# The last FFN's sums of h^T taken by token tiles ahead of its norm, and the context's turn set between the last channel products

## The chip, the core and the metric

The kernel runs on one core of a Trainium2 chip. Its time is the device time of one launch in microseconds (us). The engines are named as in the profile: PE is TensorE (PEld its weight loads), DVE VectorE, ACT ScalarE, POOL GpSimd, and SP the queue from which all transfers are issued, in a fixed order.

## The reference, cut to what matters

One layer of a diffusion backbone on 1024 latent tokens and 256 context tokens, with 1024 channels: a SwiGLU FFN, a token mixer (Fourier heads beside a two-way state-space scan, started from states that the context gives), and a second FFN. Each sublayer has a norm before and after.

```
def macaron_ffn(x, mod3, norm_pre, norm_post, w_gate, w_up, w_down):
    h = modulate(rms_norm(x, norm_pre), mod3[:, 0], mod3[:, 1])
    y = (silu(h @ w_gate) * (h @ w_up)) @ w_down
    return x + 0.5 * mod3[:, 2] * rms_norm(y, norm_post)

x, ctx = macaron_ffn(x, ...ffn1), macaron_ffn(ctx, ...ffn1)
h_f, h_b = context_states(ctx, ...)          # final scan states of the context
x = mix_sublayer(x, h_f, h_b, ...)           # input projection, conv, scan, output projection
return macaron_ffn(x, ...ffn2)
```

## The kernel before

Every fp32 operand is split into a high and a low fp32r part (ACT casts the high part, L198; DVE or POOL subtracts it for the low part, L199), and a product is three matmuls, high by high, high by low, low by high (`mm3`, L461). Tokens are worked in 8 tiles of 128. Before each large product the normed tokens are scaled, turned by PE transposes (`pre_turn`: L813, then L818 on ACT and L820 on DVE, L825 and L826 for the parts) and kept as h^T.

The order of instructions on each engine is fixed when the program is built, by a scheduler that works from its own estimate of durations; an instruction then waits only for semaphores. SP issues transfers in its own order too: a transfer that waits holds up all that stand behind it.

Two places matter here. First, `project` ends with ten channel products (`pch`, 96 matmuls of 512 columns, with convolutions L946 to L949, and for six of them transposes `pxt`, copied at L1065). After the last, `ssd_and_ctx` turns the two context tiles `cx` and starts the context's first FFN (`gu`, 256 columns), into whose steps the scan's chunks (`pcb`, `pD`, `pbt`) are mixed.

Second, `mix_out` runs over the 8 token tiles: scan, output projection (`pwo`), `post` (norm, residual, x2 written to DRAM), `pre` (norm and turn into h3, also written to DRAM as `h3_d`, L823). The last FFN's gate and up products use a seven-product scheme in place of eight for all but the first two column blocks: it needs the plain h^T blocks and four sums T1 to T4 of them. The first two blocks (weights `wfirst`) are plain products, 192 matmuls `gu`, and so can run while the sums are made. For this `ffn2` reads h3 back from DRAM (L1653 and the next line) in four chunks i through two buffers `hb`, sums (`h_sums`, L396 to L399), casts (L416) and subtracts (L422). Then `uload` (L527) brings the first weights of the scheme into a ring in the bank F0, `usums` (L534 to L537) and `usplit` prepare them, and the products `pa` to `pd` start. In the trace, F is the bank F0, h_d is h3_d, x_d is x1_d or x2_d.

Of the kernel before, what the change touches and what calls it, by code (L numbers as in the profile page):

```python
# [7 lines left out]
F32 = mybir.dt.float32  # L8
FR = mybir.dt.float32r
# [118 lines left out]
class Kernel:  # L128
# [263 lines left out]
    def h_sums(self, hb):  # L392

        m, V = self.m, self.nc.vector
        b = [m.f(hb, 512 * q, 512 * q + 512) for q in range(7)]
        V.tensor_tensor(out=b[4], in0=b[2], in1=b[3], op=ALU.add)  # L396
        V.tensor_tensor(out=b[3], in0=b[3], in1=b[0], op=ALU.subtract)
        V.scalar_tensor_tensor(out=b[5], in0=b[2], scalar=-1.0, in1=b[3], op0=ALU.mult, op1=ALU.subtract)
        V.tensor_tensor(out=b[6], in0=b[1], in1=b[5], op=ALU.add)  # L399

    def h_split(self, i, hb, highs, lows, first):

# [548 lines left out]
    def project(self):  # L951
# [90 lines left out]
        self.xs = m.alloc(8 * 768, F32, self.X)  # L1042
        acc = Ring(m, 1024, 2)
        xc = Ring(m, 1024, 2)
        cts = list(range(10, 14)) + list(range(4, 10))
        for ct in cts:
            w = self.weights(a["w_ch"][2 + ct], 1024)
            P = self.psum("pch")

            for cs in (((0, 1),) if ct != cts[-1] else ((0,), (1,))):  # L1050
                self.chan_proj(P, w, hT, cs)
            ac = m.f(acc.next())
            if ct >= 10:
                T, g = self.BT, ct - 10
                dst = m.f(T).rearrange("p (c g l) -> p c g l", g=4, l=128)[:, :, g, :]
                self.conv(P, 1024, ct, ac, dst, ac.rearrange("p (c l) -> p c l", l=128))
            else:
                x_ = m.f(xc.next())
                self.conv(P, 1024, ct, ac, x_)
                for h in range(2):  # L1060
                    P = self.psum("pxt", "D")
                    for c in range(4):
                        nc.tensor.transpose(out=P[:, 128 * c : 128 * c + 128], in_=x_[:, 512 * h + 128 * c : 512 * h + 128 * c + 128], identity=self.ident())
                    dst = m.f(self.xs).rearrange("p (c j) -> p c j", j=768)[:, 4 * h : 4 * h + 4, (ct - 4) * 128 : (ct - 4) * 128 + 128]
                    V.tensor_copy(out=dst, in_=P.rearrange("p (c j) -> p c j", j=128))  # L1065
            if ct == 10:

                self.cx, junk = [m.alloc(1024) for _ in range(2)], m.alloc(1024)
                for t in range(2):
                    self.load(self.cx[t], a["ctx"][t * 128 : t * 128 + 128, :])  # L1070
                    self.pre_scale(m.f(self.cx[t]), self.cx[t], junk)
                m.free(junk)
        acc.release()
        xc.release()
        self.whi, self.wlo = whi, wlo
        m.free(*self.hh, *self.hl)
        self.wrelease()

    def softplus(self, x, n):
# [262 lines left out]
    def ssd_and_ctx(self):  # L1342
        m, nc, a = self.m, self.nc, self.a
        V, S = nc.vector, nc.scalar
        self.rs = nc.vector
        self.y_d = self.dram([8, 128, 768], "y_d")
        self.s_d = self.dram([2, 8, 128, 768], "s_d")
        hh, hl = m.alloc(2048, FR), m.alloc(2048, FR)
        self.wrings(3, 3)
        for r in (self.whi, self.wlo):  # L1350
            r.areas = r.areas[1:] + r.areas[:1]
        full = Ring(m, 512, 2)
        for t in range(2):
            self.pre_turn(1, m.r(hh), m.r(hl), 256, t * 128, self.cx[t], full, "main")
        full.release()
        m.free(*self.cx)
# [24 lines left out]

        for j in range(NG):
            more = j < NG - 1
            self.g1_one(wa, hT, g[0], 0)
            if more:
                wa = self.weights(w1[2 * j + 2])
            slot()
            self.g1_one(wb, hT, g[1], 0)
            if more:
                wb = self.weights(w1[2 * j + 3])  # L1390
            slot()
            for t in range(2):
# [105 lines left out]
    def mix_out(self):  # L1498
# [12 lines left out]
        wo = self.wo  # L1511
        m.free(m.sub(self.ct, 0, 512))
        F0, Q = self.F0, self.Q
        yr, zr, hr = Ring(m, 768, 1, F32, F0), Ring(m, 768, 2, F32, Q), Ring(m, 768, 3, F32, Q)
        xb, x1 = Ring(m, 1024, 1, F32, F0), Ring(m, 1024, 2, F32, F0)
        Gm = self.gload(2)
        full = Ring(m, 512, 1, F32, F0)
        tr, ft = Ring(m, 384, 3, F32, F0), Ring(m, 256, 1, F32, Q)
# [69 lines left out]
        full.areas.append(m.alloc(512, F32, F0))  # L1588
        P = xx = None
        for c in range(8):  # L1590
            fo, f0 = fr.next(), ft.next()
# [21 lines left out]

        (X1, X2) = self.cut("x", (12288, FR), (1536, F32))
        self.X1, self.X2 = X1, X2
        self.whi, self.wlo = Pairs(), Pairs()
        for b in (R0, X1):
            for r in (self.whi, self.wlo):
                r.areas.append(m.alloc(2048, FR, b))
        self.raw = Ring(m, 1024, 3, F32, Q)  # L1620
        w1 = a["ffn2_w1"]
        self.wfirst = [self.weights(w1[0]), self.weights(w1[1])]
        (h0, l0), (h1, l1) = h3
        gu = self.psum("gu")
        for half in range(2):
            for k in range(8):
                self.g_half_k(gu, self.wfirst[0], ((h0, h1), (l0, l1), 512), 0, k, (half,))
        self.gfirst = gu
        pre(7, post(7, P))
        for r in (xb, x1, full, self.raw):  # L1630
            r.release()
        m.free(Gm)
        (self.Q,) = self.cut("q", (Q_WORDS, FR))


    def ffn2(self):
# [20 lines left out]

        s0 = m.alloc(1024, F32, F0)
        self.banks(main=4)
        hT = ((h0, h1), (l0, l1), 512)  # L1660
        for c in range(2):
            for q in range(2):
                P = self.gfirst if (c, q) == (0, 0) else self.psum("gu")
                if (c, q) != (0, 0):
# [7 lines left out]
        m.free(s0, *hb)  # L1672
# [15 lines left out]
        def tail():  # L1688
# [6 lines left out]
            self.gring.areas = [tuple(m.sub(x, o, 384) for x in T[0]) for o in (0, 384)]  # L1695
# [4 lines left out]
        self.ffn_up(False, tail)  # L1700
        for r in (self.ut, self.sg):
            r.release()
        m.free(self.cc, wb, lb, h0, l0, h1, l1, *(x for q in T[1:] for x in q), *(m.sub(x, 768, 1280) for x in T[0]))
# [131 lines left out]
```

## Time and profile before

| | us |
|---|---|
| median of 3 runs | 2336.15 (2334.01 to 2337.88) |
| the profiled execution, its own time | 2346.82 |
| its span in the trace | 2344.8 |
| PE busy | 2168.8, 92% of the span |
| DVE / ACT / POOL busy | 1505.1 / 924.3 / 422.6 |

The span is read from the first instruction to the last; 2.0 us of the execution lie around it. PE's idle time is 176 us, and the mean granted clock is 0.966.

### The profile page before, as it was taken

The page shows a single profiled execution, that of the slowest core. Times are in us where ns is not written, and L with a number is a line of the kernel's source. Part 1 is how long each engine was busy: PE and PEld are TensorE (multiplying, and loading weights), DVE is VectorE, ACT ScalarE, POOL GpSimd, SP SyncE. Part 2 cuts the span into 40 slices and gives each one's busy share as a digit, 9 for nine tenths or more (in the row PEclk, how much of TensorE's full clock was granted, in tenths as well). Part 3 has the DMA queues.
Part 4 walks back from the last instruction along what each step waited for, and adds up shares of the span by engine and source line. Part 5 has one row for each costly group of instructions (what it writes and reads, how often), then busy time and mean ns, then how long its engine had stood idle before and what let it go on. Part 6 is the DMA issues. An engine that isn't in the chain of part 4 may idle for free. (4 is left out here: it accounts for less than half of the span.)

```text
span 2344.8 us, 28370 instructions
## 1 busy us (share of the span) xinstructions
PE 2168.8 (92%) x10532; PEld 1805.8 (77%) x10532; DVE 1505.1 (64%) x2226; ACT 924.3 (39%) x1403; POOL 422.6 (18%) x444
## 2 busy tenths in 40 slices
PE   5799999999999899998899987888799999999998
PEld 3577778887778799887888877666688888878886
DVE  6999886656645513348887866787556565656453
ACT  4322223234535433326556545356222222245341
POOL 1100000000212000007776631673000000001010
PEclk9799999999999999999999989999899999999999
DMA  6344553228755501312455445453412222258572
GB/s 259 112 136 153 169 175 99 96 84 276 251 181 192 174 28 47 105 46 90 139 165 178 145 135 166 136 182 122 153 57 85 77 87 75 88 185 275 180 228 88
DMA packets 124827, 329.39 MB, mean 140 GB/s; under 512 B 12928, under 2 KB 43776, under 8 KB 123664
## 3 DMA queue, kind: packets, MB, share of 16 engines
q1 hardware_dynamic: 124688, 327.57, 42.8%
q8 instruction: 83, 1.36, 0.2%
q14 instruction: 56, 0.46, 0.1%
HBM read 273.77 MB, written 53.76 MB: 140 GB/s over the span
## 5 line engine op out<-in xcount | busy, mean ns | idle before, releaser
L198 ACT CAST R<-F 128x1024 fp32r<-128x1024 f32 (+1 forms) x172 | 164.3, 961 | 242.5 <-PE pd L461 75.1
L199 DVE TENSOR_TENSOR R<-F,R 128x1024 fp32r<-128x1024 f32 (+1 forms) x155 | 196.3, 1271 | 79.4 <-ACT R L198 72.7
L207 POOL TENSOR_SCALAR F<-F 128x1 f32<-128x1 f32 x18 | 4.2, 235 | 1279.7 <-ACT F L228 1279.7
L198 ACT CAST Q1a<-F 128x1024 fp32r<-128x1024 f32 (+1 forms) x115 | 129.3, 1130 | 225.8 <-PE pd L461 102.7
L461 PE MATMUL pch<-R 128*128 128x512 f32 (+1 forms) x912 | 172.2, 349 | 13.8 <-DVE X3b L790 4.7
L461 PEld LDWEIGHTS pch<-R 128*128 128x128 f32 x912 | 148.1, 198 | 33.9 <-issue 10.3
L461 PE MATMUL gu<-R 128*128 128x256 f32 (+1 forms) x1152 | 162.2, 299 | 2.7 <-ACT R L198 1.2
L461 PEld LDWEIGHTS gu<-R 128*128 128x128 f32 x1152 | 149.8, 194 | 11.2 <-ACT R L198 1.6
L199 DVE TENSOR_TENSOR Q1a<-F,Q1a 128x1024 fp32r<-128x1024 f32 x93 | 113.5, 1220 | 39.0 <-ACT Q1a L198 38.8
L1253 POOL TENSOR_TENSOR R<-F 128x384 fp32r<-128x384 f32 x128 | 128.6, 1033 | 24.2 <-PE pD L1287 17.5
L461 PE MATMUL y<-Q1a 128*128 128x512 f32 x438 | 107.7, 395 | 0.0
L461 PE MATMUL pa<-R,Q1a 128*128 128x512 f32 x330 | 95.6, 401 | 10.9 <-ACT Q1a L198 9.6
L461 PE MATMUL pa<-R 128*128 128x512 f32 x306 | 87.5, 403 | 14.1 <-ACT R L198 13.3
L461 PE MATMUL y<-Q1a,X3a 128*128 128x512 f32 x360 | 93.2, 404 | 5.5 <-DVE X3b L790 2.6
L768 DVE SCALAR_TENSOR_TENSOR X3b<-X3b,F 128x512 f32<-128x512 f32 x126 | 95.1, 770 | 4.2 <-DMA X3b<-adaR 3.9
L461 PEld LDWEIGHTS y<-Q1a 128*128 128x128 f32 x438 | 83.3, 191 | 18.2
L198 ACT CAST X7a<-F 128x1024 fp32r<-128x1024 f32 (+1 forms) x47 | 57.8, 1231 | 90.9 <-PE pd L461 78.5
L461 PE MATMUL pc<-R,Q1a 128*128 128x512 f32 x286 | 87.6, 401 | 0.7 <-DVE F L604 0.7
L461 PEld LDWEIGHTS y<-Q1a,X3a 128*128 128x128 f32 x360 | 68.9, 193 | 22.9 <-issue 3.0
L461 PE MATMUL pd<-R,Q1a 128*128 128x512 f32 x286 | 84.9, 393 | 0.0
L461 PEld LDWEIGHTS pa<-R,Q1a 128*128 128x128 f32 x330 | 62.1, 191 | 29.1 <-ACT Q1a L198 12.1
L199 DVE TENSOR_TENSOR X7a<-F,X7a 128x1024 fp32r<-128x1024 f32 (+1 forms) x47 | 68.1, 1451 | 24.7 <-ACT X7a L198 24.6
(424 smaller groups left out, 4911.1 us busy)
## 6 DMA issues: line engine op xcount, KB each, us to landing
F<-ffn_wd SPq DMA_DIRECT2D x154, 512.0 KB, 4.3
F<-ffn_w SPq DMA_DIRECT2D x42, 1024.0 KB, 5.4
X3b<-adaR SPq DMA_DIRECT2D x112, 256.0 KB, 2.9
F<-ffn_w SPq DMA_DIRECT2D x44, 512.0 KB, 4.4
F<-w_ch SPq DMA_DIRECT2D x26, 512.0 KB, 4.1
g_d<-X3b SPq DMA_DIRECT2D x22, 512.0 KB, 2.7
g_d<-F SPq DMA_DIRECT2D x20, 512.0 KB
X3b<-g_d SPq DMA_DIRECT2D x44, 192.0 KB, 5.8
```

Of the source, the lines that this page charges most:

```text
L198: nc.scalar.copy(out=m.r(hi, off, off + n), in_=m.f(src, soff, soff + n))
L199: (E or nc.vector).tensor_tensor(out=m.r(lo, off, off + n), in0=m.f(src, soff, soff + n), in1=m.f(hi, off, off + n), op=ALU.subtract)
L207: V.tensor_scalar(out=mv, in0=ss, scalar1=scale * RSQ_M, scalar2=EPS * RSQ_M, op0=ALU.mult, op1=ALU.add)
L461: self.nc.tensor.matmul(out=outs[c], lhsT=l, rhs=r[c], start=first and ps == 0, stop=last and ps == 2, skip_group_check=again)
L768: V.scalar_tensor_tensor(out=ac, in0=m.f(x), scalar=s, in1=ac, op0=ALU.mult, op1=ALU.add)
L1253: G.tensor_tensor(out=m.r(R, 384 * i, 384 * i + 384).rearrange("p (h l) -> p h l", h=3), in0=self.cst(tri).unsqueeze(1).broadcast_to([128, ...
```

## The change

The context tiles are loaded and scaled before the channel products. The last two channel products are done for the first 512 tokens, then the first half of h^T is freed, the turned context takes its room, and the second 512 tokens follow; the turn stands between them.

In `mix_out`, the sums T1 to T4 are formed there, for the first three token tiles of each half (384 columns) through one buffer of five areas, and for the last pair (tiles 3 and 7) straight from the turn's buffers. The raw weights of the first two blocks come through one area in the bank X2 (X7b) and one in F0, since Q holds the sums. The second block's first product is done here too. The diff, cut to its core:

```diff
+    def t_sums(self, b):
+        V = self.nc.vector
+        V.tensor_tensor(out=b[4], in0=b[2], in1=b[3], op=ALU.add)
+        V.tensor_tensor(out=b[3], in0=b[3], in1=b[0], op=ALU.subtract)
+        V.scalar_tensor_tensor(out=b[2], in0=b[2], scalar=-1.0, in1=b[3], op0=ALU.mult, op1=ALU.subtract)
+        V.tensor_tensor(out=b[1], in0=b[1], in1=b[2], op=ALU.add)
+    def t_split(self, T, src, q, c, n):
...
+        nc.scalar.copy(out=hi, in_=src)
+        nc.vector.tensor_tensor(out=lo, in0=src, in1=hi.bitcast(F32), op=ALU.subtract)
     def project(self):
...
+        self.cx, junk = [m.alloc(1024) for _ in range(2)], m.alloc(1024)
+        for t in range(2):
+            self.load(self.cx[t], a["ctx"][t * 128 : t * 128 + 128, :])
+            self.pre_scale(m.f(self.cx[t]), self.cx[t], junk)
...
+        last = [(ct, self.weights(a["w_ch"][2 + ct], 1024), self.psum("pch")) for ct in cts[-2:]]
+        for ct, w, P in last:
+            self.chan_proj(P, w, hT, (0,))
+        m.free(self.hh[0], self.hl[0])
+        self.chh, self.chl = m.alloc(2048, FR), m.alloc(2048, FR)
+        self.cw = m.alloc(2048, FR), m.alloc(2048, FR)
+        full = Ring(m, 512, 2)
+        for t in range(2):
+            self.pre_turn(1, m.r(self.chh), m.r(self.chl), 256, t * 128, self.cx[t], full, "CB")
...
+        for ct, w, P in last:
+            self.chan_proj(P, w, hT, (1,))
+            conv(ct, P)
     def ssd_and_ctx(self):
...
-        for t in range(2):
-            self.pre_turn(1, m.r(hh), m.r(hl), 256, t * 128, self.cx[t], full, "main")
     def mix_out(self):
...
+        self.T = [(m.alloc(2048, FR, b), m.alloc(2048, FR, b)) for b in (self.Q, self.Q, X1, X1)]
-        self.raw = Ring(m, 1024, 3, F32, Q)
+        self.raw = Ring(m, 1024, 1, F32, X2)
+        self.raw.areas.append(m.alloc(1024, F32, F0))
         w1 = a["ffn2_w1"]
         self.wfirst = [self.weights(w1[0]), self.weights(w1[1])]
...
+        self.gfirst = [self.psum("gu")]
+        first(0, 0)
+        first(0, 1)
+        hb = m.alloc(5 * 384, F32, F0)
+        for i in range(4):
+            v = m.f(hb).rearrange("p (q c) -> p q c", c=384)
+            nc.sync.dma_start(out=v[:, 0:4:3], in_=self.h3_d[4 + i].rearrange("p (s c) -> p s c", s=2)[:, :, 0:384])
+            nc.sync.dma_start(out=v[:, 1:3], in_=self.h3_d[i].rearrange("p (s c) -> p s c", s=2)[:, :, 0:384])
+            self.t_sums([v[:, q] for q in range(5)])
+            self.t_split(self.T[i], v[:, 1:5], 0, 0, 384)
+        m.free(hb)
+        hb = m.alloc(3 * 512, F32, X2)
+        for q, k in ((0, 4), (1, 0)):
+            nc.sync.dma_start(out=m.f(hb, 512 * q, 512 * q + 512).rearrange("p (k c) -> p k c", k=4),
+                              in_=self.h3_d[k : k + 4, :, 384:512].rearrange("k p c -> p k c"))
+        xx = post(7, P)
+        self.gfirst.append(self.psum("gu"))
+        first(1, 0)
+        f = [full.areas[(full.i + q) % 2] for q in range(2)]
+        pre(7, xx)
+        b = [m.f(hb, 0, 512), m.f(hb, 512, 1024), m.f(f[0]), m.f(f[1]), m.f(hb, 1024, 1536)]
+        self.t_sums(b)
+        for i in range(4):
+            for q in range(4):
+                self.t_split(self.T[i], b[1 + q][:, 128 * i : 128 * i + 128].rearrange("p (q c) -> p q c", q=1), q, 384, 128)
+        first(1, 1)
     def ffn2(self):
...
-        T = [(m.alloc(2048, FR, b), m.alloc(2048, FR, b)) for b in (Q, Q, X1, X1)]
-        hb = [m.alloc(3584, F32, F0) for _ in range(2)]
         for i in range(4):
-            b = hb[i % 2]
-            nc.sync.dma_start(out=m.f(b, 0, 2048).rearrange("p (s c) -> p s c", s=4)[:, 0:4:3, :], in_=self.h3_d[4 + i].rearrange("p (s c) -> p s c", s=2))
-            self.load(b, self.h3_d[i], 512, 1536)
-            self.h_sums(b)
-            self.h_split(i, b, [(3, 7, T[i][0])], [(3, 7, T[i][1])], 3)
+            for q, op in enumerate(("T4", "T2", "T1", "T3")):
+                self.hop[op][i] = at(T[i][0], q), at(T[i][1], q)
```

The order in which instructions stand, before and in the change (built, not run). PE, end of the channel products and start of the context's FFN, before:

```order
L461 MATMUL pch<-R_60 128x512 x45
L1063 MATMUL pxt<-F_61 128x128 x8
L461 MATMUL pch<-R_60 128x512 x5
L813 MATMUL ptr<-F_61,X5a 128x128 x4
L1267 MATMUL pcb<-Q4a,X5a 128x128 x4
L813 MATMUL ptr<-F_61,X5a 128x128 x8
L1063 MATMUL pxt<-F_61,X5a 128x128 x8
L813 MATMUL ptr<-F_61,X5a 128x128 x4
L1287 MATMUL pD<-R_60 128x384 x4
L461 MATMUL gu<-R_60 128x256
L1287 MATMUL pD<-R_60 128x384 x5
L461 MATMUL gu<-R_60 128x256 x11
```

The same place in the change:

```order
L477 MATMUL pch<-R_60 128x512 x17
L829 MATMUL ptr<-F_61,X5a 128x128 x4
L477 MATMUL pch<-R_60 128x512 x28
L829 MATMUL ptr<-F_61,X5a 128x128 x4
L477 MATMUL pch<-R_60 128x512 x7
L477 MATMUL gu<-R_60 128x256 x12
L1080 MATMUL pxt<-F_61 128x128 x8
L1300 MATMUL pcb<-Q4a,X5a 128x128 x4
L477 MATMUL gu<-R_60 128x256 x40
L1080 MATMUL pxt<-F_61,X5a 128x128 x8
L477 MATMUL gu<-R_60 128x256 x23
```

The four groups of transposes `ptr` stood behind the last `pch`; the last two of them now stand within the last products (the other two stand earlier), and `gu` follows the last `pch` at once.

SP, from the last writes of h3 to the first weights of the scheme (L527), before:

```order
L823 DMA h_d<-F_61 128x4x128 x3
L1653 DMA F_61<-h_d 128x2x512 x2
L1671 DMA g_d<-F_61 128x512
L184 DMA F_61<-h_d 128x1024 x2
L184 DMA X7b<-g_d 128x256
L1653 DMA F_61<-h_d 128x2x512 x2
L184 DMA F_61<-h_d 128x1024
L1671 DMA g_d<-F_61 128x512
L184 DMA F_61<-h_d 128x1024
L184 DMA X7b<-g_d 128x256
L527 DMA F_61<-ffn_w 128x2x1024 x2
L1671 DMA g_d<-F_61 128x512
```

The same stretch in the change, from the last write of h3 (L839 now); L1669 and L1670 are a chunk's two loads, L1725 the writes of the first two blocks' result, L543 the former L527:

```order
L839 DMA h_d<-F_61 128x4x128
L184 DMA X7b<-g_d 128x256
L1669 DMA F_61<-h_d 128x2x384
L184 DMA X7b<-g_d 128x256
L1670 DMA F_61<-h_d 128x2x384
L1725 DMA g_d<-F_61 128x512
L1669 DMA F_61<-h_d 128x2x384
L1670 DMA F_61<-h_d 128x2x384
L1725 DMA g_d<-F_61 128x512
L543 DMA F_61<-ffn_w 128x2x1024 x4
```

Before, two chunks' loads stood side by side and the weights stood ahead of the last two result writes; now a chunk's loads stand alone, and the weights stand behind all four chunks and all result writes. The first chunk's loads stand above this stretch, before the last tile's two writes of h3.

DVE, the last chunk's sums (L396 to L399, subtraction L422), the first blocks' gate times up (L1670) and the scheme's weight sums (L534 to L537), before:

```order
L398 SCALAR_TENSOR_TENSOR F_61<-F_61 128x512
L399 TENSOR_TENSOR F_61<-F_61 128x512
L422 TENSOR_TENSOR X7a<-F_61,X7a 128x2048
L1670 TENSOR_TENSOR F_61<-gu,F_61 128x512
L422 TENSOR_TENSOR X7a<-F_61,X7a 128x2048
L534 TENSOR_TENSOR F_61<-F_61 128x1024
L536 TENSOR_TENSOR F_61<-F_61 128x512
L537 TENSOR_TENSOR F_61<-F_61 128x512
L199 TENSOR_TENSOR R_60<-F_61,R_60 128x1024 x2
L534 TENSOR_TENSOR F_61<-F_61 128x1024
L199 TENSOR_TENSOR X7a<-F_61,X7a 128x1536
L1670 TENSOR_TENSOR F_61<-gu,F_61 128x512
```

The same place in the change (sums L404 to L407, subtraction L415; L1724 multiplies gate and up, L550 is the former L534):

```order
L407 TENSOR_TENSOR F_61<-F_61 128x384
L1724 TENSOR_TENSOR F_61<-gu,F_61 128x512
L415 TENSOR_TENSOR X7a<-F_61,X7a 128x4x384
L1724 TENSOR_TENSOR F_61<-gu,F_61 128x512
L404 TENSOR_TENSOR F_61<-F_61 128x384
L405 TENSOR_TENSOR F_61<-F_61 128x384
L406 SCALAR_TENSOR_TENSOR F_61<-F_61 128x384
L407 TENSOR_TENSOR F_61<-F_61 128x384
L415 TENSOR_TENSOR X7a<-F_61,X7a 128x4x384
L550 TENSOR_TENSOR F_61<-F_61 128x1024
```

The fourth chunk now stands behind the last multiplication of the first blocks, and the scheme's weights behind the fourth chunk. Before, the last chunk and the first weights stood ahead of the last multiplication.

## Rows read from the trace of the kernel before

**Rows 1.** The page, part 1: busy us, share of the span, instructions.

```profile
PE 2168.8 (92%) x10532; PEld 1805.8 (77%) x10532; DVE 1505.1 (64%) x2226; ACT 924.3 (39%) x1403; POOL 422.6 (18%) x444
```

**Rows 2.** Windows: length; busy us of PE, PEld, DVE, ACT, POOL; clock; DMA share, GB/s.

```profile
960.00:1060.00 100.00, 100.00 (x459) 83.18 (x458) 41.53 (x44) 32.79 (x31) 3.71 (x4) 1.00 0.17 52
1072.00:1090.00 18.00, 12.28 (x72) 10.41 (x73) 15.90 (x29) 6.66 (x12) 11.11 (x11) 0.81 0.19 62
1675.00:1688.00 13.00, 0.00 (x0) 0.00 (x0) 9.40 (x9) 5.40 (x6) 0.00 (x0) 0.59 0.53 181
```

**Rows 3.** Timeline of PE, 1040 to 1100: start, us, what, idle before it.

```profile
1072.70 0.72 PE L813 MATMUL ptr<-F,X5a 128*128 128x128 f32 x4 [4.31 <-DVE X5a L820]
...
1076.04 1.08 PE L813 MATMUL ptr<-F,X5a 128*128 128x128 f32 x4 [2.63 <-DVE F L948]
...
1083.07 0.41 PE L1287 MATMUL pD<-R 128*128 128x384 f32 x1 [1.03 <-ACT F L1292]
...
1086.48 6.30 PE L461 MATMUL gu<-R 128*128 128x256 f32 x49 [1.05 <-DVE X5a L820]
```

**Rows 4.** Timeline of DVE, same stretch.

```profile
1074.02 0.68 DVE L826 TENSOR_TENSOR R<-X5a,R 128x512 fp32r<-128x512 f32 x1
1074.62 1.27 DVE L948 SCALAR_TENSOR_TENSOR F<-pch,F 128x1023 f32<-128x1023 f32 x1
```

**Rows 5.** Timeline of PE, 1612 to 1705.

```profile
1618.10 0.62 PE L461 MATMUL pwo<-X6a,R 128*128 128x512 f32 x2
...
1663.29 11.40 PE L461 MATMUL gu<-R,X7a 128*128 128x512 f32 x48
1688.04 1.22 PE L461 MATMUL pa<-R 128*128 128x512 f32 x2 [13.34 <-ACT R L198]
```

**Rows 6.** Chain of waits, 1612 to 1710: start us, us, what.

```profile
1620.21 1.05 ACT R L198
...
1621.28 1.24 DVE R L199
...
1622.54 4.30 DMA Q4a<-ffn_w
...
1641.61 2.29 DMA h_d<-F
...
1661.77 3.63 DMA F<-h_d
...
1665.42 5.29 DMA F<-h_d
...
1678.46 6.17 DMA F<-ffn_w
...
1684.73 1.24 DVE F L534
```

**Rows 7.** Timeline of DVE, ACT and SP, 1612 to 1705.

```profile
1612.38 0.55 DVE L1572 TENSOR_TENSOR R<-Q4a,R 128x384 fp32r<-128x384 f32 x1
...
1631.42 1.06 ACT L228 ACTIVATE F<-F 128x1024 f32<-128x1024 f32 x1 [2.51 <-DVE F L791]
...
1634.65 1.15 ACT L803 ACTIVATE F<-F 128x1024 f32<-128x1024 f32 x1
1634.71 7.27 SPq L823 DMA_DIRECT2D h_d<-F  x3
...
1637.08 0.46 ACT L818 ACTIVATE F<-ptr,F 128x128 f32<-128x128 f32 x1 [0.77 <-DVE F L820]
...
1652.57 0.69 DVE L396 TENSOR_TENSOR F<-F 128x512 f32<-128x512 f32 x1 [7.26 <-DMA F<-h_d]
...
1687.89 1.47 ACT L198 CAST X7a<-F 128x1536 fp32r<-128x1536 f32 x1
...
1690.73 1.75 DVE L199 TENSOR_TENSOR X7a<-F,X7a 128x1536 fp32r<-128x1536 f32 x1
```

**Rows 8.** DMA issues, 1430 to 1720: KB each, median us to landing.

```profile
F<-y_d SPq DMA_DIRECT2D x8, 384.0 KB, 2.9
```

More of the change, by code (lines that the diff above doesn't have):

```diff
@@ L399, in h_sums @@
         V.tensor_tensor(out=b[6], in0=b[1], in1=b[5], op=ALU.add)
+    def t_sums(self, b):
[5 more added lines that the diff above has]
+    def t_split(self, T, src, q, c, n):
+        nc = self.nc
+        k = src.shape[1]
+        hi, lo = (x[0].view[FR][:, x[1] + 512 * q : x[1] + 512 * (q + k)].rearrange("p (q c) -> p q c", c=512)[:, :, c : c + n] for x in T)
+        nc.scalar.copy(out=hi, in_=src)
+        nc.vector.tensor_tensor(out=lo, in0=src, in1=hi.bitcast(F32), op=ALU.subtract)
     def h_split(self, i, hb, highs, lows, first):
@@ L1044, in project, with conv @@
         xc = Ring(m, 1024, 2)
[L1045 to L1051, printed above, removed]
+        self.cx, junk = [m.alloc(1024) for _ in range(2)], m.alloc(1024)
+        for t in range(2):
+            self.load(self.cx[t], a["ctx"][t * 128 : t * 128 + 128, :])
+            self.pre_scale(m.f(self.cx[t]), self.cx[t], junk)
+        m.free(junk)
+        def conv(ct, P):
             ac = m.f(acc.next())
@@ L1065, in project @@
                     V.tensor_copy(out=dst, in_=P.rearrange("p (c j) -> p c j", j=128))
-            if ct == 10:
-                self.cx, junk = [m.alloc(1024) for _ in range(2)], m.alloc(1024)
-                for t in range(2):
-                    self.load(self.cx[t], a["ctx"][t * 128 : t * 128 + 128, :])
-                    self.pre_scale(m.f(self.cx[t]), self.cx[t], junk)
-                m.free(junk)
+        cts = list(range(10, 14)) + list(range(4, 10))
+        for ct in cts[:-2]:
+            w = self.weights(a["w_ch"][2 + ct], 1024)
+            P = self.psum("pch")
+            self.chan_proj(P, w, hT, (0, 1))
+            conv(ct, P)
[8 more added lines that the diff above has]
+            self.pre_turn(1, m.r(self.chh), m.r(self.chl), 256, t * 128, self.cx[t], full, "CB")
+        full.release()
+        m.free(*self.cx)
+        for ct, w, P in last:
+            self.chan_proj(P, w, hT, (1,))
+            conv(ct, P)
         acc.release()
@@ L1075, in project @@
         self.whi, self.wlo = whi, wlo
-        m.free(*self.hh, *self.hl)
+        m.free(self.hh[1], self.hl[1])
         self.wrelease()
@@ L1347, in ssd_and_ctx @@
         self.s_d = self.dram([2, 8, 128, 768], "s_d")
[L1348 to L1353, printed above, removed]
-            self.pre_turn(1, m.r(hh), m.r(hl), 256, t * 128, self.cx[t], full, "main")
-        full.release()
-        m.free(*self.cx)
+        hh, hl = self.chh, self.chl
+        self.wrings(3, 2)
+        for r, x in ((self.whi, self.cw[0]), (self.wlo, self.cw[1])):
+            r.areas.insert(0, x)
         hT = ([hh], [hl], 256)
@@ L1513, in mix_out @@
         F0, Q = self.F0, self.Q
-        yr, zr, hr = Ring(m, 768, 1, F32, F0), Ring(m, 768, 2, F32, Q), Ring(m, 768, 3, F32, Q)
+        full = Ring(m, 512, 1, F32, F0)
+        Gm = self.gload(2)
+        yr, tr = Ring(m, 768, 1, F32, F0), Ring(m, 384, 2, F32, F0)
+        tr.areas.append(m.alloc(384, F32, F0, True))
         xb, x1 = Ring(m, 1024, 1, F32, F0), Ring(m, 1024, 2, F32, F0)
-        Gm = self.gload(2)
-        full = Ring(m, 512, 1, F32, F0)
-        tr, ft = Ring(m, 384, 3, F32, F0), Ring(m, 256, 1, F32, Q)
+        zr, hr, ft = Ring(m, 768, 2, F32, Q), Ring(m, 768, 3, F32, Q), Ring(m, 256, 1, F32, Q)
         self.h3_d = self.dram([8, 128, 1024], "h3_d")
@@ L1587, in mix_out @@
         z = scan(0)
-        full.areas.append(m.alloc(512, F32, F0))
+        full.areas.append(m.alloc(512, F32, F0, True))
         P = xx = None
@@ L1615, in mix_out @@
         self.X1, self.X2 = X1, X2
+        (self.Q,) = self.cut("q", (Q_WORDS, FR))
         self.whi, self.wlo = Pairs(), Pairs()
@@ L1619, in mix_out @@
                 r.areas.append(m.alloc(2048, FR, b))
-        self.raw = Ring(m, 1024, 3, F32, Q)
+        self.T = [(m.alloc(2048, FR, b), m.alloc(2048, FR, b)) for b in (self.Q, self.Q, X1, X1)]
+        self.raw = Ring(m, 1024, 1, F32, X2)
+        self.raw.areas.append(m.alloc(1024, F32, F0))
         w1 = a["ffn2_w1"]
         self.wfirst = [self.weights(w1[0]), self.weights(w1[1])]
+        self.raw.release()
         (h0, l0), (h1, l1) = h3
-        gu = self.psum("gu")
-        for half in range(2):
+        hT = ((h0, h1), (l0, l1), 512)
@@ L1626, in mix_out, with first @@
+        def first(q, half):
             for k in range(8):
[L1627 to L1630, printed above, removed]
+                self.g_half_k(self.gfirst[q], self.wfirst[q], hT, 0, k, (half,))
+        self.gfirst = [self.psum("gu")]
[8 more added lines that the diff above has]
+            self.t_split(self.T[i], v[:, 1:5], 0, 0, 384)
@@ L1631, in mix_out @@
+        self.t_sums(b)
[3 more added lines that the diff above has]
+        first(1, 1)
+        for r in (xb, x1, full):
             r.release()
-        m.free(Gm)
-        (self.Q,) = self.cut("q", (Q_WORDS, FR))
+        m.free(Gm, hb)
     def ffn2(self):
@@ L1648, in ffn2 @@
             self.hop["B22"][i] = at(h1, i), at(l1, i)
-        T = [(m.alloc(2048, FR, b), m.alloc(2048, FR, b)) for b in (Q, Q, X1, X1)]
-        hb = [m.alloc(3584, F32, F0) for _ in range(2)]
+        T = self.T
         for i in range(4):
-            b = hb[i % 2]
-            nc.sync.dma_start(out=m.f(b, 0, 2048).rearrange("p (s c) -> p s c", s=4)[:, 0:4:3, :], in_=self.h3_d[4 + i].rearrange("p (s c) -> p s c", s=2))
-            self.load(b, self.h3_d[i], 512, 1536)
-            self.h_sums(b)
-            self.h_split(i, b, [(3, 7, T[i][0])], [(3, 7, T[i][1])], 3)
+            for q, op in enumerate(("T4", "T2", "T1", "T3")):
+                self.hop[op][i] = at(T[i][0], q), at(T[i][1], q)
         s0 = m.alloc(1024, F32, F0)
@@ L1662, in ffn2 @@
             for q in range(2):
-                P = self.gfirst if (c, q) == (0, 0) else self.psum("gu")
-                if (c, q) != (0, 0):
+                P = self.psum("gu") if c else self.gfirst[q]
+                if c:
                     for half in range(2):
@@ L1671, in ffn2 @@
                 nc.sync.dma_start(out=self.g_d[q][:, 512 * c : 512 * c + 512], in_=s)
-        m.free(s0, *hb)
+        m.free(s0)
         (wa, la), (wb, lb) = self.wfirst
@@ L1693, in tail @@
             self.wring.areas = [tuple(self.wq["A11"]), tuple(self.wq["S1"])]
-            self.gring.areas = [tuple(m.sub(x, o, 384) for x in T[0]) for o in (0, 384)]
+            self.gring.areas = [tuple(m.sub(x, o, 384) for x in T[0]) for o in (512, 896)]
             self.down_begin("ffn2", ((0, 1), (2, 3, 4), (5, 6, 7)))
@@ L1702, in ffn2 @@
             r.release()
-        m.free(self.cc, wb, lb, h0, l0, h1, l1, *(x for q in T[1:] for x in q), *(m.sub(x, 768, 1280) for x in T[0]))
+        m.free(self.cc, wb, lb, h0, l0, h1, l1, *(x for q in T[1:] for x in q), *(m.sub(x, 0, 512) for x in T[0]), *(m.sub(x, 1280, 768) for x in T[0]))
         self.pairs(Q, 2, 0)
```

## The prediction, made before the changed kernel ran

> **What bounds the kernel now.** I read the page's busy times first: PE works 2168.8 us, 92% of the span, so what a change can move here is PE's idle time (176 us) or its clock [rows 1]. The windows come next, to see where PE stops in the two places that the change touches [rows 2]. In 960 to 1060 PE is busy all of the time at the full clock, and DVE only 41.53 of 100 us: work added on DVE there is hidden. In 1072 to 1090, where the context is turned, PE is busy 12.28 of 18 us at a clock of 0.81, and DVE 15.90 of 18. In 1675 to 1688, before the scheme's first products, PE does nothing at all. The timeline of PE then gives each wait and its releaser [rows 3, 5], the chain of waits what the second one is made of [rows 6], and the timelines of the other engines the single durations [rows 4, 7].
>
> **First place: the turned context.** Behind the last channel product PE waits 4.31 and 2.63 us before two groups of transposes, 1.03 before `pD` and 1.05 before the context's first FFN [rows 3]: 9.0 us, which the change takes away, since the transposes stand between channel products and `gu` follows the last one at once. What is late next is the low half of the turned context. On DVE it stands, by the order, behind three subtractions of 1024 columns and two halves of a convolution. These take 3 x 1.24 [rows 6] + 2 x 1.27 + 0.68 for the half itself [rows 4] = 6.9 us after the last product. PE has beside it 12 `gu` (6.30 / 49 = 0.13 each [rows 3], 1.5 us), then 8 `pxt` and 4 `pcb`, which I take at 0.2 us each from the four `ptr` in 0.72 to 1.08 [rows 3]: 2.4 us. The new wait is 6.9 - 3.9 = 3.0 us, and the place gives 9.0 - 3.0 = 6.0 us. Bounds: if DVE gets there in time and the clock stays full, 9.0 + 0.19 x 12.28 = 11.3 us [rows 2]; if PE's cover is gone, because DVE starts that much later, 9.0 - 6.9 = 2.1 us. I take the middle, 6.0, which uses each row as it stands. The loads and the scaling of the context go to where DVE has over half its time free, and the scan's `pcb`, `pD`, `pbt` only change their turn among steps of the same work: both at nothing; if DVE were not free there, the scaling of two tiles would cost some 2 us.
>
> **Second place: from the last token tiles to the scheme.** Before, PE's 192 plain products end at 1663.29 + 11.40 = 1674.7, and the first scheme product starts at 1688.04 after 13.34 us of waiting [rows 5]. What ends that wait is a chain: the last h3 write landing at 1641.61 + 2.29 = 1643.9, the four chunks (the last pair's loads are 1661.77 + 3.63 and 1665.42 + 5.29), the weights issued at 1678.46, which take 6.17, their sum from 1684.73, casts [rows 6]. From there to the first product it is 1688.04 - 1678.46 = 9.6 us, and from the write's landing to the weights 34.5 us. The change keeps the 192 products and this last 9.6 us, and changes what lies between. I follow it from its start.
>
> The raw weights of the first blocks come through areas that must come free. The one in X7b is part of what `pwo` reads until 1618.10 + 0.62 = 1618.7 [rows 5]. A load of 4.30, a cast of 1.05 and a subtraction of 1.24 [rows 6] follow, and the second load into the same area waits for that subtraction: 1618.7 + 2 x 6.6 = 1631.9. Its cast stands on ACT ahead of the last tile's norm, which before runs from 1631.42 to 1634.65 + 1.15 = 1635.8 [rows 7], 4.4 us, and so ends at 1636.3. Tile 6's last turned half needs another 0.46 on ACT [rows 7] and about as much on DVE, so its h3 write is issued at 1637.2 and lands 2.29 later, at 1639.5 [rows 6]. That is 4.4 us before the last write's landing of before: the gain of working only three of four tiles from DRAM. Lower bound for it: where before issues its last writes, 1634.71 [rows 7] + 2.29 = 1637.0, so 2.5 us earlier.
>
> From there the four chunks run through one buffer. Each load of the next waits for the subtraction that reads the buffer last, and the second load of a chunk waits for its first, as the pair of before did (1661.77 + 3.63 = 1665.40, and the next starts at 1665.42 [rows 6]). A round is two loads of 384 KB, four sums of 384 columns, one cast and one subtraction of 1536 columns. The trace has no such load of h3. Three quarters of the 512 KB loads of before are 0.75 x 3.63 = 2.7 and 0.75 x 5.29 = 4.0 [rows 6], and 384 KB of y take 2.9 [rows 8]; I take 3.4, the middle of the first two, since both loads are of h3 and the queue carries other transfers beside them. The sums are 4 x 0.55 = 2.2, the cast 1.47, the subtraction 1.75 [rows 7], and some 0.3 for issue: 6.8 + 2.2 + 1.5 + 1.7 + 0.3 = 12.5 us, four rounds 50.0. The last pair's four sums of 512 columns (0.69 each, 2.8 [rows 7]) stand on DVE within the second round; 2.0 of it I count, the rest beside a load. Its 16 small casts and subtractions lie beside loads too, at nothing; the rows of before have none of 128 columns, and if each took half of the 384-column 0.55, they would add up to 4.4 us on one engine. So the chunks end at 1639.5 + 52.0 = 1691.5.
>
> The weights L543 cannot go earlier: on SP they stand behind all chunks' loads and all four result writes, and their first area in F0 is one that the chunks' buffer uses. With the 9.6 us from weights to product, the scheme starts at 1691.5 + 9.6 = 1701.1, 13.1 us later than before. PE's cover is spent at about 1674.7 as before, so all of it is idle time: 26.4 us instead of 13.34. Bounds: eight loads at 2.9 and a start at 1637.0 give 13.1 - 8 x 0.5 - 2.5 = 6.6 us; eight loads at 4.0 give 13.1 + 4.8 = 17.9.
>
> The fit of the Trainium skill for one transfer, 2.0 us and bytes over 436 GB/s ("DMA: Bandwidth & Descriptors", section "Anatomy of one DMA — SWDGE (gpsimd) path"), would give 2.9 us for 393 KB and 3.2 for 524 KB, each an estimate. The y loads agree with it [rows 8], the h3 loads at 3.63 and 5.29 are above it [rows 6]; by the page the sum for this place would be 4.0 us less.
>
> **The sum.** -6.0 + 13.1 = +7.1 us. The profiled execution took 2346.82 us (span 2344.8 and 2.0 around it), and would be 2353.9; the median of the timed runs is 10.7 lower, and I move it by the same: 2336.15 + 7.1 = 2343.2.
>
> **Rivals.** *Quick loads.* The chunks' loads take 2.9 like those of y, since no chunk of another buffer is in flight beside them: second place 13.1 - 4.0 = 9.1, in all +3.1, 2339.3. For it: before, the slower of a pair, 5.29, ran while the weights and results were also in the queue. Against: the 3.63 of 512 KB ran alone and is already above the y rate.
>
> *The other side: the two loads of a chunk run side by side.* They fill areas 0 and 3, and 1 and 2, so nothing in the data makes the second wait. Then each round loses one load, 4 x 3.4 = 13.6 us, the second place comes to -0.5, and with the first place the kernel is at -6.5: 2329.7. It decides from the point where the second load of a chunk starts before the first lands. Against it: before, areas cut in the same way were loaded one behind the other [rows 6], and between the two loads of some chunks other transfers stand on SP.
>
> *Worse on both.* Loads at 4.0 as the 5.29 says, with the first place at 4 to 6: 17.9 - 5 = about +13, 2349. For it: the first chunks' loads share the queue with writes of h3, x2 and of the results.
>
> *The change doesn't do what it says.* By the order only the first chunk's sums stand ahead of the last tile's turn, and the fourth stands behind the last of the plain products; that is part of the forecast. If the engines nevertheless get three chunks done by 1674.7, the place ends near +3, and the time is that of the quick loads.
>
> **How the numbers follow.** Forecast 0.50, from 2340 to 2347; quick loads, with the last rival, 0.25; side by side 0.12; worse 0.13. What a measurement of this kernel tells from no change is 0.2%, 4.7 us: below 2331.5 is faster, above 2340.8 slower. The forecast lies above that for nearly nine tenths of its share (0.44), "worse" wholly (0.13); quick loads lie within, save some 0.03 on either side; side by side is faster in 0.09, the first place giving less in the rest. Together about 0.12 faster, 0.32 same, 0.56 slower; since two bounds of the first place could fall on the good side, I write 0.13, 0.33 and 0.54. The range: both places at their better bounds give -11.3 + 6.6 = -4.7 (2331.5), both at the worse -2.1 + 17.9 = +15.8 (2352). I take 2331 to 2350.5; the forecast's own range is 2340 to 2347.
>
> **What would show it.** First place: `gu` directly behind the last `pch`, and one wait of 2 to 4 us before `gu` that DVE ends. Second place: chunks' first loads starting near 1639 less what the first place gave; loads of 3.4 in single file; the weights issued 52 us later; PE idle some 26 us before the first `pa`. It is wrong if the two loads of a chunk overlap, if the weights land before the last chunk is split, or if PE's wait before `pa` is under 18 us.

## The result

The changed kernel takes 2362.74 us, the median of 4 runs (2358.91 to 2366.21), against 2337.02 for the one before: ratio 1.0102, 95% interval 1.0067 to 1.0137. Timed again in turn with more runs of the one before it is 1.0097 (1.0083 to 1.0111), 22.7 us. That is slower, as forecast, but three times the 7.1 us of the forecast and above its range. The profiled execution of the change took 2358.91, the quickest of its four, and that of before 2346.82, near the slowest of its own: the two traces differ by 12.1 us of their times.

The page after has PE's work unchanged against [rows 1]:

```profile
PE 2169.1 (92%) x10532; PEld 1806.4 (77%) x10532; DVE 1512.2 (64%) x2246; ACT 924.3 (39%) x1417; POOL 423.1 (18%) x444
```

**The second place** went much as worked out. The timeline of PE (start, us, what, idle before it), answering [rows 5], shows that the plain products end at 1681.4 and the scheme starts 21.77 us later.

```profile
1673.07 8.35 PE L477 MATMUL gu<-R,X7a 128*128 128x512 f32 x35
1703.19 1.22 PE L477 MATMUL pc<-Q8a,R 128*128 128x512 f32 x2 [21.77 <-ACT R L198]
```

The chain of waits after, answering [rows 6], shows the two loads of a chunk one behind the other, the chunks too, and the weights behind the last one:

```profile
1669.40 3.30 DMA F<-h_d
...
1672.71 3.39 DMA F<-h_d
...
1681.85 3.35 DMA F<-h_d
...
1685.22 3.84 DMA F<-h_d
...
1691.55 1.48 ACT X7a L414
...
1693.05 1.77 DVE X7a L415
...
1694.84 5.97 DMA F<-ffn_w
...
1700.83 1.24 DVE F L550
```

The second load of each chunk starts when the first has landed; the loads take 3.3 to 3.9 us (3.4 taken). The four rounds take 13.1, 15.2, 12.4 and 13.0 us (12.5 each taken, and 2.0 more for the last pair's sums, which stand in the second): 53.7 instead of 52.0. The first chunk's loads start at 1641.1, the weights are issued at 1694.84.

**The first place.** The timeline of PE after, answering [rows 3]: `gu` follows the last `pch`, and the one wait left there is 3.52 us (3.0 worked out). The last row shown is new: the context's down products `y` wait 6.28 us for VectorE; before, the same four started at 1100.43 without a wait.

```profile
1064.52 1.86 PE L477 MATMUL pch<-R 128*128 128x512 f32 x7
1066.47 1.67 PE L477 MATMUL gu<-R 128*128 128x256 f32 x12
...
1073.60 6.41 PE L477 MATMUL gu<-R 128*128 128x256 f32 x39 [3.52 <-DVE R L842]
...
1100.48 1.22 PE L477 MATMUL y<-R 128*128 128x512 f32 x2 [6.28 <-DVE R L199]
```

Further on, two pairs of rows of PE (`y`, then `pdft`) stand for what happens to the lead. Before:

```profile
1155.71 2.08 PE L461 MATMUL y<-R 128*128 128x512 f32 x4 [3.15 <-ACT R L198]
...
1387.88 6.74 PE L1228 MATMUL pdft<-Q4a,X5a 128*128 128x256 f32 x16 [5.36 <-DMA Q4a<-dft]
```

After:

```profile
1150.97 2.08 PE L477 MATMUL y<-R 128*128 128x512 f32 x4 [2.81 <-ACT R L198]
...
1193.24 6.36 PE L477 MATMUL gu<-R 128*128 128x256 f32 x35 [4.79 <-DVE X5a L528]
...
1233.88 0.91 PE L1357 MATMUL pst<-Q4a 128*128 128x384 f32 x2 [3.00 <-DVE F L1345]
...
1393.81 6.47 PE L1261 MATMUL pdft<-Q4a,X5a 128*128 128x256 f32 x17 [5.54 <-DMA Q4a<-dft]
```

At 1151 the change is 4.74 us ahead, at 1394 5.9 us behind: 10.7 us are lost between. The table follows single matmuls (the same one of the same tile) through the traces; the numbers are us later than before, and the headings give each one's time there. The lower rows are runs described under Experiments.

| trace | channel products (1045.6) | context FFN (1178.7) | its end (1281.0) | token tiles (1600.2) | scheme (1738.9) |
|---|---|---|---|---|---|
| changed | -1.2 | -4.8 | +5.4 | +0.9 | +13.1 |
| changed, again | -0.2 | -3.9 | +6.5 | +5.9 | +19.4 |
| new turn alone | +1.8 | -0.9 | +13.1 | +10.2 | +10.2 |
| new sums alone | -0.6 | -0.6 | -0.3 | -2.4 | +10.6 |
| sums mended | -1.4 | -1.0 | -1.7 | -1.5 | -6.6 |
| turn, half of GpSimd's rows | +4.4 | -5.8 | -9.2 | -14.4 | -14.7 |
| its base | +0.5 | -10.7 | -12.9 | -21.7 | -19.5 |

**Where the lead goes: waits and clock.** Windows from the second point of the table to the third and on to the fourth: length; busy us of PE, PEld, DVE, ACT, POOL; mean granted clock; DMA share, GB/s. Before:

```profile
1178.69:1281.07 102.38, 97.20 (x663) 87.99 (x662) 87.66 (x123) 62.42 (x110) 73.96 (x61) 1.00 0.53 169
1281.07:1600.23 319.16, 275.54 (x1501) 234.89 (x1500) 243.46 (x519) 164.35 (x335) 163.71 (x142) 0.93 0.48 153
```

The change, and behind it the second stretch of the change again:

```profile
1173.94:1286.48 112.54, 101.62 (x672) 92.77 (x670) 93.00 (x122) 59.64 (x108) 80.78 (x72) 0.95 0.48 152
1286.48:1601.14 314.66, 271.45 (x1501) 230.66 (x1500) 240.87 (x519) 165.11 (x337) 161.94 (x142) 0.95 0.49 152
...
1287.62:1606.09 318.47, 274.30 (x1501) 232.74 (x1500) 241.99 (x519) 164.87 (x337) 161.40 (x142) 0.93 0.47 150
```

In the first stretch the change loses 10.2 us. PE's idle time in it grows by 5.7 us, from 5.2 to 10.9. The other 4.4 are PE's busy time: nine more matmuls lie between the two points, and the granted clock is 0.50 (1.2 GHz) from 1190.8 to 1197.6 and 0.51 from 1235.1 to 1238.5, behind the waits of 4.79 and 3.00 us, where before it is 1.00 (2.4 GHz) throughout.

**What VectorE lost.** The groups of the scan's multiply-adds (96 in two groups; count, then busy us, mean ns, idle before), L1299 before:

```profile
L1299 DVE SCALAR_TENSOR_TENSOR F<-X5a,F 128x128 f32<-128x128 f32 x78 | 37.7, 536 | 0.4
...
L1299 DVE SCALAR_TENSOR_TENSOR X5a<-X5a,F 128x128 f32<-128x128 f32 x18 | 11.3, 668 | 0.2
```

and the same instructions after, L1332:

```profile
L1332 DVE SCALAR_TENSOR_TENSOR F<-X5a,F 128x128 f32<-128x128 f32 x78 | 47.5, 663 | 0.4
...
L1332 DVE SCALAR_TENSOR_TENSOR X5a<-X5a,F 128x128 f32<-128x128 f32 x18 | 12.5, 743 | 0.5 <-ACT X5a L1331 0.5
```

49.0 us have become 60.0 for the same work. (The expectations below say 54 and 65: there each instruction's own duration is added, overlaps twice.) Ahead of the 6.28 us wait seven of them take 7.11 us:

```profile
1088.02 7.11 DVE L1332 SCALAR_TENSOR_TENSOR F<-X5a,F 128x128 f32<-128x128 f32 x7
```

How that comes about is seen just before the 4.79 us wait. VectorE after, 1186 to 1194:

```profile
1186.71 0.86 DVE L1332 SCALAR_TENSOR_TENSOR F<-X5a,F 128x128 f32<-128x128 f32 x3
...
1187.96 4.09 DVE L1332 SCALAR_TENSOR_TENSOR F<-X5a,F 128x128 f32<-128x128 f32 x3
1191.98 1.21 DVE L528 TENSOR_TENSOR X5a<-y,X5a 128x1024 f32<-128x1024 f32 x1
```

GpSimd in the same stretch:

```profile
1187.30 1.43 POOL L1286 TENSOR_TENSOR R<-F 128x384 fp32r<-128x384 f32 x1 [1.12 <-PE pD L1320]
1188.69 2.38 POOL L199 TENSOR_TENSOR R<-F,R 128x1024 fp32r<-128x1024 f32 x1
1191.04 3.32 POOL L1286 TENSOR_TENSOR R<-F 128x384 fp32r<-128x384 f32 x4
```

GpSimd waits until 1187.30. The three multiply-adds that start at 1186.71 take 0.86 us, the next three, beside GpSimd's subtraction and its decay rows (L1286, the scan's products of 384 columns), 4.09; L528, which frees the bank that PE waits for, stands behind them. Over the whole stretch those with no GpSimd work beside them take 0.34 us on average in either kernel (61 before, 45 after), the others 0.94 before and 0.97 after, and all that take over 0.6 us (33 before, 41 after) run beside GpSimd. The Trainium skill ("SBUF — State Buffer", section "SBUF: two separate sides") says that an operation of VectorE with two inputs in SBUF and one of GpSimd that reads SBUF hold a shared pair of ports in turn, the other being blocked for the whole instruction. These rows agree, with 0.34 us alone and up to 2.5 us beside GpSimd.

### The profile page after: what moved, and what is told of

The parts are those of the page before. It is cut to its first block, busy times and chain, and to the rows that moved or that the text cites. A ratio compares the mean times of both kernels' runs of the same rounds, so it can differ in the third digit from the quotient of the medians.

```text
span 2357.0 us, 28404 instructions
## 1 busy us (share of the span) xinstructions
PE 2169.1 (92%) x10532; PEld 1806.4 (77%) x10532; DVE 1512.2 (64%) x2246; ACT 924.3 (39%) x1417; POOL 423.1 (18%) x444
## 5 line engine op out<-in xcount | busy, mean ns | idle before, releaser
L477 PE MATMUL gu<-R 128*128 128x256 f32 (+1 forms) x1152 | 171.9, 309 | 13.9 <-DVE X5a L528 6.4
L477 PEld LDWEIGHTS gu<-R 128*128 128x128 f32 x1152 | 157.0, 201 | 25.0 <-DVE X5a L528 7.8
L1286 POOL TENSOR_TENSOR R<-F 128x384 fp32r<-128x384 f32 x128 | 127.5, 1024 | 24.8 <-PE pD L1320 17.1
```

Source lines behind the costliest of these rows:

```text
L477: self.nc.tensor.matmul(out=outs[c], lhsT=l, rhs=r[c], start=first and ps == 0, stop=last and ps == 2, skip_group_check=again)
L1286: G.tensor_tensor(out=m.r(R, 384 * i, 384 * i + 384).rearrange("p (h l) -> p h l", h=3), in0=self.cst(tri).unsqueeze(1).broadcast_to([128, ...
```

## Experiments

Ratios are to the kernel before, timed in turn with the run on the same chip (its medians 2340 to 2342), with 95% intervals. Differences in us are worked out from the ratios, or from two medians where both runs were timed together.

**The change again.**

> The changed kernel as it is, timed in turn with the one before on one chip. The two profiled executions differ by 12.1 us, the medians by 25.7. Theory 1, the cost is what the traces show (place two +12, place one nothing in the end): ratio 1.005 to 1.006. Theory 2, the timed runs carry something that the profiled execution of before (2346.82, the slowest of its four) already had: ratio about 1.010, and the executions of before lie near 2336.

2363.65 us, 1.0097 (1.0083 to 1.0111): theory 2. The trace says where single executions part: both traces of the change are 5 to 7 us behind at 1281, but in the token tiles the first gives 4.5 of it back and this one 0.7. The windows above show what that is: PE idles 43 to 44 us there in all three traces, but is busy 271.45 us at a mean clock of 0.95 in the first, 274.30 and 275.54 at 0.93 in this one and before. One pair of profiles was not enough for a difference of 10 us.

**The turn alone.**

```diff
     def project / ssd_and_ctx: as in the change
     def mix_out / ffn2: as before
```

> The kernel before with the first part of the change alone: the context loaded and turned between the channel products, the last FFN's sums as before. Theory 1 (first place gives some 5 us and the scan mixed with the context's FFN takes them back before the token tiles): PE ahead by 4 to 5 us at the context's down products, 0 to 6 behind at the end of that FFN, total within 4 us of before. Rival, the forecast's own term: 6 us faster, about 2330.

2353.00 us, 1.0050 (1.0035 to 1.0065), 11.7 slower. Both the -6 and the "within 4" fall. The lead is there at 1179 (2.7 us against its own start, table), and it is 13.1 behind at 1281; the token tiles give 2.9 back.

**The sums alone.**

> The kernel before with the second part of the change alone: sums by token tiles through one buffer, context turned as before. Theory 1: PE idle 26 to 29 us before the first scheme product and all of the loss here, +12 to +13 us, ratio 1.005. Theory 2 (the timed loss is all of this part): +24, ratio 1.010. Rival (the two parts need each other): within 5 us of before.

2355.07 us, 1.0058 (1.0041 to 1.0075), 13.6 slower: theory 1. The two parts add up: 11.7 + 13.6 = 25.3, where 22.7 is measured for both.

**The weights clear of the chunks' buffer.**

```diff
-        self.raw = Ring(m, 2560, 2, F32, F0)
-        self.we = m.alloc(1024, F32, F0)
+        self.we = m.alloc(1024, F32, F0, True)
...
+        self.raw.areas = [m.alloc(2560, F32, F0, True) for _ in range(2)]
```

> The changed kernel, with the scheme's raw weights placed at the top of F0, clear of the chunks' buffer and of the first blocks' results; nothing else. Theory (weights wait for the buffer's last chunk): the first weights are issued well before the last chunk's split, the 6 us of their load go from the path, and the first scheme product starts 6 to 8 us earlier, ratio 0.997 to the changed kernel. Rival (the last chunk's sums bound the products anyway, or the weights' load lengthens the chunks' loads): under 3 us.

2355.62 us, 1.0063 (1.0049 to 1.0076), 8.0 less than the change timed beside it. On PE the first products start 2.63 us behind the plain ones, and then wait for the chunks, the last of which is loaded at 1690.72 instead of 1681.85:

```profile
1686.98 3.03 PE L477 MATMUL pa<-R 128*128 128x512 f32 x12 [2.63 <-DVE F L1724]
...
1704.50 0.80 PE L477 MATMUL pb<-X7a,R 128*128 128x512 f32 x1 [5.70 <-ACT X7a L414]
```

The gain is of the theory's size, though not in its way: the first product is 16.2 us earlier, not 6 to 8, and the rival's mechanism, later chunks, takes half of that back.

**Loads that don't interleave.** In this run and the next two, the rings of the down products overwrite one block of T4 of the first chunk before the last unit reads it; the instructions are the same in kind and number.

```diff
...
-            ... out=v[:, 0:4:3], in_=self.h3_d[4 + i] ...
-            ... out=v[:, 1:3], in_=self.h3_d[i] ...
-            self.t_sums([v[:, q] for q in range(5)])
+            ... out=v[:, 0:2], in_=self.h3_d[4 + i] ...
+            ... out=v[:, 2:4], in_=self.h3_d[i] ...
+            self.t_sums([v[:, q] for q in (0, 2, 3, 1, 4)])
...
```

> The changed kernel, with the chunks' buffer laid out so that each of a chunk's two loads fills one unbroken stretch (areas 0 and 1, areas 2 and 3) instead of areas 0 and 3 beside 1 and 2; the blocks of T come in another order for it. Theory (the second load waits for the first because their areas interleave): the second load is issued while the first is on its way, each round loses about 3 us, four rounds 10 to 12, ratio 0.995 to 0.996 of the changed kernel. Rival (it waits for the queue or for the buffer, not for the first load): within 2 us of the changed kernel.

2357.76 us, 1.0077 (1.0064 to 1.0091), some 5 us less than the change. SP's queue shows the second load 0.6 us behind the first:

```profile
1672.14 0.53 SPq L1669 DMA_DIRECT2D F<-h_d  x1
1672.72 0.61 SPq L1670 DMA_DIRECT2D F<-h_d  x1
...
1684.35 0.53 SPq L1669 DMA_DIRECT2D F<-h_d  x1
1684.97 0.56 SPq L1670 DMA_DIRECT2D F<-h_d  x1
...
1695.31 0.39 SPq L543 DMA_DIRECT2D F<-ffn_w  x1
```

So the interleaving was the wait. It gave half of the 10 to 12: in the last three rounds, 11.0 to 12.2 us long, a load takes 4.1 (median) instead of 3.6, and the second weights wait behind a result write (chain of waits):

```profile
1695.87 5.50 DMA g_d<-F
...
1701.45 4.83 DMA F<-ffn_w
```

**Both edits; and both with the old turn.**

> Both edits on the changed kernel: loads that don't interleave, and the raw weights clear of the chunks' buffer. Theory (chunks and weights are the whole of the second place's loss): the first scheme product within 5 us after the last plain product, 16 to 20 us ahead of the changed kernel, so that what is left against before is the first place's loss, +3 to +8 us, ratio 1.001 to 1.003. Rival (transfers collide once they run side by side): no more than the better of the two edits alone, some 12 us.

2349.31 us, 1.0038 (1.0024 to 1.0052): some 14 less than the change, more than either edit, and 9 above before, a little more than the +3 to +8 expected for the first place's loss. The first scheme product follows the last plain one at once, at 1686.7.

> The kernel before with the second part of the change and both edits, the context turned as before. Theory (the second place, mended, ends before's 13 us wait, the first part costs 7 to 11): 4 to 8 us faster than before, ratio 0.997 to 0.998. Rival (first place gains in this company, or the queue's order eats the gain): no faster than before.

2337.49 us, 0.9983 (0.9973 to 0.9994): 4 faster. The two differ in the turn alone: 11.8 us.

**The same, with the block of T4 left whole.**

```diff
-            self.gring.areas = [... for o in (512, 896)]
+            self.gring.areas = [... for o in (0, 1024)]
...
```

> As the run with the second part, both edits and the old turn, with the areas for the down products' first blocks moved off a block of T that the last unit still reads. Theory: 3 to 5 us faster than before, ratio 0.998, and the first scheme product within 5 us of the last plain one. Rival: the earlier gain hung on that block and goes, within 1 us of before.

2336.98 us, 0.9981 (0.9969 to 0.9993), 4 us faster than before by the ratio, 3 by the medians: of the kernels here that compute everything, the one with the lowest ratio. Its first scheme products follow the plain ones with no wait:

```profile
1671.06 8.82 PE L477 MATMUL gu<-R,X7a 128*128 128x512 f32 x37
1679.72 2.92 PE L477 MATMUL pa<-R 128*128 128x512 f32 x12
```

**A third of the multiply-adds.**

```diff
+                    if r == 0:
                         V.scalar_tensor_tensor(out=w, in0=..., in1=w, op0=ALU.mult, op1=ALU.add)
```

> The kernel before, leaving out two of every three of the scan's multiply-adds on VectorE (of each group's three heads only the first is combined): 64 of 96, some 36 us of VectorE's work between 1090 and 1340. It is the base for the next run. If VectorE holds up that stretch, 3 to 12 us faster than before; if not, within 2 us.

> The first part of the change alone, with the same two of three multiply-adds left out. In the traces the 96 multiply-adds take 53.8 us before and 65 in every trace with the new turn, all of the difference in those that run beside GpSimd (0.34 us alone, 0.9 to 1.1 beside it). Theory (the loss of the first place is VectorE's, made by these collisions): with a third of them left the turn keeps its gain, 1 to 6 us faster than the run without it. Rival (the loss comes from the other order of products and the lower clock after the waits, not from the multiply-adds): still 7 to 11 us slower than the run without it.

The base takes 2336.94 us, 0.9987 (0.9971 to 1.0003); the turn 2333.23, 0.9971 (0.9961 to 0.9981): 3.7 faster by the medians, with intervals that overlap, where it was 11.7 slower with all of them. The loss needs the multiply-adds. The base gains no more than 3 us by 36 us less work on VectorE: without the turn VectorE hardly held up this stretch.

**The multiply-adds off VectorE, nothing left out.**

```diff
-                    V.scalar_tensor_tensor(out=w, ...)
+                    S.activation(out=W2[r], in_=cb[512 + ...], func=AF.Copy, scale=...)
+                V.tensor_tensor(out=m.f(W), in0=m.f(W), in1=m.f(W2), op=ALU.add)
...
```

> The changed kernel with both edits of the second place, and the scan's 96 multiply-adds taken off VectorE whole: ScalarE scales the second factor too (96 more of its scalings, 0.39 us each), VectorE adds three heads in one sum of 384 columns (32 at about 0.55), with one area less in the ring of the products to make room. Nothing is left out. Theory (the multiply-adds beside GpSimd are what the new turn loses by): it is 1 to 6 us faster than the next run, where the same pair with the multiply-adds on VectorE was 12 us slower, and the fastest of all, ratio 0.994 to 0.997. Rival (the order of products and the clock): still 7 to 12 us slower than the next run.

> The same with the old turn of the context: the base for the run above. Against the mended second place alone (ratio 0.998), theory and rival both leave it within 5 us: VectorE has some 20 to 35 us less to do in that stretch, and ScalarE 37 more.

With the turn 2339.66 us, 0.9997 (0.9985 to 1.0009); without 2338.82, 0.9988 (0.9975 to 1.0001). The 11.8 us between such a pair have gone to 0.8: the rival's 7 to 12 fall, but so do the gain of 1 to 6 and the ratio of 0.994 to 0.997 that the theory expected. The one without the turn is no faster than with the multiply-adds on VectorE (0.9981 above). In the first 40 us the theory is plain: the wait before `y` is 0.83, not 6.28.

```profile
1100.29 1.18 PE L477 MATMUL y<-R 128*128 128x512 f32 x4 [0.83 <-DVE R L199]
```

**Half of GpSimd's decay rows, VectorE whole.**

```diff
+                if i % 2 and Rr.i > 2:
+                    continue
                 G.tensor_tensor(out=m.r(R, 384 * i, 384 * i + 384)...
```

> The kernel before, leaving out the low parts of the scan's decay rows on GpSimd after the first two groups (about 60 of 128 products of 384 columns; old rows are used again in their place). VectorE's work is whole. It is the base for the next run. If the collisions cost before something too (54 us for 96 multiply-adds that would take 33 alone), up to 6 us faster than before.

> The first part of the change alone, with the same of GpSimd's work left out. Collision theory: the multiply-adds fall from 65 to some 50 us, near those of its base, and the turn's loss of 11 us falls to under 5. Amount theory (VectorE has too much to do whatever GpSimd does) and order theory: the turn is still 7 to 12 us slower than its base.

Of the 128 products on GpSimd 68 are left. The base takes 2325.19 us, 0.9935 (0.9921 to 0.9949), 15.8 less than before and far more than the 6 expected at most; the turn 2319.67, 0.9917 (0.9901 to 0.9933). The turn's loss of 11.7 is gone; 5.5 faster by the medians, though the intervals of the two ratios overlap. The multiply-adds, of the base and of the turn:

```profile
L1301 DVE SCALAR_TENSOR_TENSOR F<-X5a,F 128x128 f32<-128x128 f32 x78 | 29.6, 431 | 0.3
...
L1301 DVE SCALAR_TENSOR_TENSOR X5a<-X5a,F 128x128 f32<-128x128 f32 x18 | 6.4, 401 | 0.6 <-ACT X5a L1300 0.5
```

```profile
L1318 DVE SCALAR_TENSOR_TENSOR F<-X5a,F 128x128 f32<-128x128 f32 x78 | 32.4, 468 | 0.3
...
L1318 DVE SCALAR_TENSOR_TENSOR X5a<-X5a,F 128x128 f32<-128x128 f32 x18 | 9.8, 588 | 0.1
```

VectorE has the same instructions as before in both, and they take 36.0 and 42.2 us instead of 49.0 and 60.0: it is the company of GpSimd, not the amount. Nor is it the order of PE's products: the scheduler orders anew when work is left out, but from 1046 to 1281 this turn keeps 1336 of the 1377 matmuls of the turn alone in the same order (told by the tile they write and their columns), and the loss is gone. These two runs also take GpSimd's own delay away (PE waited 1.5 us for its rows in the change, 3.9 in the turn alone), so not all of the 15.8, nor of the 11.7, is shown to be the multiply-adds'.

## Why the prediction was wrong

**Second place, right.** +13.1 was worked out, 13.6 measured with the sums alone. Loads in single file, weights behind the last chunk and the load time hold, though part of the closeness is luck: in the trace of the change the chunks start 1.6 us later than worked out and take 1.7 longer, and the way from the weights to the product is 8.4 us instead of 9.6. The lower bound for the start read a row of three writes (1634.71 [rows 7]) as the last of them, which was issued at 1641.61 [rows 6]; only the better bound, 6.6, uses it. For the rest, the side-by-side rival was rightly refused, and the cause given against it (areas cut alike) is the one that the edit removed. PE's idle time was 21.8 instead of 26 us because its plain products ended 6.7 us later as well (1681.4 against 1674.7), which the forecast did not have; the scheme's start, 1703.2 against 1701.1, is what counts. The quick loads of 2.9 us, a rival, did not come: no load of the change took under 3.3.

**First place, wrong in one step.** It is the term put at nothing: "the scan's `pcb`, `pD`, `pbt` only change their turn among steps of the same work". The waits removed and the new wait were right (3.52 against 3.0), and PE was 4 to 5 us ahead at 1179. But with PE earlier at the context's FFN, the scan's chunks ran later beside it, on VectorE at the times when GpSimd worked on the same chunks: 11 us more for the same 96 instructions, handed to PE as waits of 6.28, 4.79 and 3.00, each with a stretch at half the clock (0.50 from 1091.8 to 1105.4 around the first). I had read VectorE's 15.90 of 18 us as a queue that sets one wait; VectorE was late in the stretch that follows too. The bound of 11.3 us counted on a full clock, but between the first two points of the table the mean is 0.91, against 0.95 before. -6.0 was +11.7. With 11.7 in its place the sum would have been 24.8, against 22.7.

**From profile to median.** The forecast took the profiled executions to lie the same way off their medians. The profile of before was 5 to 11 us above, that of the change 4 to 5 below. This is not what failed, but the traces alone, 12.1 us apart, would have made the forecast look near.

What stays open: why the clock is granted more in the token tiles of some executions than of others, and how the turn's loss divides between VectorE's multiply-adds and GpSimd's own rows. With the multiply-adds on ScalarE the turn's lead does appear, 5.1 us up to the second point of the table, and 4.1 are lost again by the third, where PE waits 7.1 us before the scan's `pst`, against 4.1 without the turn; why is open too.

## What to carry to other kernels

A stall of the busiest engine may be worth nothing where the engine beside it uses the time to catch up: before a stall is counted as gain, add up that engine's work to the end of the stage. When work is moved, ask which two engines it will newly run beside each other, not only what it waits for. And here a buffer that interleaved two loads' areas made them follow one another, and a ring put where a late buffer lay made its load late: edits of addresses turned 13.6 us of loss into 4 of gain.

## What the runs showed of the hardware

A multiply-add of 128 columns on VectorE takes 0.34 us alone and 0.94 to 0.97 on average beside GpSimd. Leaving out half of GpSimd's decay rows made the kernel 15.8 us faster, though GpSimd is busy 18% of the span; in this stretch, 1046 to 1281 before, it is busy 166 of 235 us.
